# Low parts behind attention: from two engines to VectorE alone

## The chip, the cores and the metric

The kernel runs on one core of a Trainium2 chip. The metric is the device time of one execution in microseconds (us), as a median of several runs. A core has TensorE (PE, with its weight loads shown as PEld), VectorE (DVE), ScalarE (ACT), GpSimd (POOL) and SyncE (SP), which here only starts DMAs. Each engine takes its instructions in order.

## The reference, cut to what matters

One decoder block over 2048 positions of width 1024. The part that the change touches is the end: the output projection of the attention branch, the merge of the two branches, and the last projection.

```python
y_rnn = (hr * silu(z_rnn)) @ w_out_rnn
y_attn = (o * silu(z_attn)) @ w_out_attn
merged = sigmoid(g_r + bg_r) * y_rnn + sigmoid(g_a + bg_a) * y_attn
x = x + gate * (merged @ w_o)
return rms_norm(x, g_final)
```

## The kernel before, in words

**Split operands.** Every float32 operand of a matmul is held as a high part and a low part. ACT rounds the value to the high part (`hi_act`, L158). The low part is value minus high part, one elementwise subtraction on 128x512 elements, either on POOL (`lo_pool`, L164) or on DVE (`lo_dve`, L167). A product is then three matmuls (`mm3`, all on L150): high weight by high data, high weight by low data, low weight by high data, in that order.

**The jobs.** `steps` is a generator that runs eight jobs. Jobs 0 to 3 multiply `w_out_rnn` with the recurrent branch `yaT`, jobs 4 to 7 multiply `w_out_attn` with the attention branch `oT`; a job takes 512 positions. A job has 8 tiles of output rows (`t` counts them from 0 to 63, `m` within a job), a tile has 8 steps (`k`), and a step is one `mm3`, so a tile is 24 matmuls. The weights of a tile come in two halves, numbered `x = 2t` and `2t + 1`. Up to `t = 39` the steps are spread between the matmuls of attention. The last three jobs, `t = 40` (`TAIL0`) to `63`, come behind attention and are what this case is about: they take 192 steps (`LAST`).

**What a tile needs there.** The halves `x > 81` (`RAW`) are loaded unsplit from `wR` by SP (`load_w`, L1675) into one of six buffers, named S0 to S3, st3 and st4, five halves ahead; at the third step of half `x`, so six steps ahead of its use, `split_w(x + 2)` puts a `hi_act` on ACT and a low part on DVE (even `x`) or POOL (odd `x`). `split_y` does the same for the eight 128x512 blocks of `oT` of the next job; from job 6 on they are emitted around the steps given in `LATE_SPLIT_Y`, the last two of them in the first tile of the job that uses them. `evict` of tile `t - 1` comes in the second step of tile `t`: DVE multiplies the sum in PSUM with the gate block (L1716) and adds the recurrent branch's block (L1718); the two blocks are loaded by L1710 and the result is stored to `meT` by L1724, both on SP. The sums have two PSUM buffers, so tile `t + 1` can't start until tile `t - 1` is evicted.

**The output weights' rows.** The last projection is done afterwards by seven products for each pair of rows (`output_pair`), with operands B11, T2, T3, T1, B21, T4, B22 built from `w_o` while the last three jobs run. `build_rows(s, k)` is called for `s` = 14, 72, 100, 142 with `k` = 0 to 3 and hangs work on the steps `s` to `s + 21`: two products with the gate vector on POOL, four combinations on DVE, seven high parts on ACT and seven low parts. The rows come 512 KB at a time, two loads for each `k`, ten and seven steps before `s`; for `k` of 1 to 3 ACT's queue starts them, and each has to wait until the rows that lie in the same buffer (those of `k - 1`) have been read for the last time. The helpers:

```python
def load_rows(k, i):                                                      # L1852
    v[k, i] = t = stage(1 + i, [P, D])
    (nc.scalar if k else nc.sync).dma_start(t[:], w_o[...])               # L1854
def gate_rows(k, i):
    nc.gpsimd.tensor_tensor(v[k, i][:], v[k, i][:], v["gate"][:], ALU.mult)  # L1857
def combine(name, k, a, b, op):
    tt(part(name, k), part(a, k), part(b, k), op)                         # L1865, DVE
def low(name, k, lo):
    lo(B[name][1][:, k, :], part(name, k), B[name][0][:, k, :])           # L1871
```

T1, T2, T3 and T4 are made in place of B22, B11, B12 and B21 of the same rows, each from a difference or a sum of two parts. The whole stage is written out in emission order by hand (`manual_schedule`), so an engine's queue is the order of the code: within a step first the loads, the weight splits and the eviction, then the matmuls, then the splits of `oT`, and last what `build_rows` hung on the step.

Of the kernel before, what the change touches and what calls it, by code (L numbers as in the profile page):

```python
# [24 lines left out]
NB = 4  # L25
# [64 lines left out]
def decoder_block(ctx, tc, x, c, positions, g_norm, w_mod, b_mod, w_in, b_gate, conv_w, conv_b,  # L90
# [4 lines left out]
    def T(pool, shape, dt, tag, **kw):  # L95
        cnt[0] += 1
        return pool.tile(shape, dt, tag=tag, name=f"{tag}_{cnt[0]}", **kw)
# [59 lines left out]
    def hi_act(o, i):  # L157
        nc.scalar.activation(o, i, AF.Copy)  # L158
# [7 lines left out]
    def lo_dve(o, i, h):  # L166
        return nc.vector.tensor_tensor(o, i, h.bitcast(F32), ALU.subtract).ins  # L167
# [166 lines left out]
    n_w, n_y, W, Y0 = [0], [0], {}, {}  # L334
# [1323 lines left out]
    def steps(jobs):  # L1658
# [18 lines left out]
        def split_w(x):  # L1677
            if RAW < x < 2 * len(tiles):
                raw = W[x][:, 1].bitcast(F32)
                hi_act(W[x][:, 0], raw)  # L1680
                (lo_pool if x % 2 else lo_dve)(W[x][:, 1], raw, W[x][:, 0])

        def load_y(j, k, t):
            if j < len(jobs):
# [10 lines left out]
        def split_y(j, k):  # L1695
            if j < len(jobs):
                Y[j, k] = yh, yl = [T(fl, [P, CH], F32R, tag, bufs=NY) for tag in ("yh", "yl")]
                w, ys, n = jobs[j]
                t = Y0.pop((ys is yaT, n, k))
                hi_act(yh[:], t[:])  # L1700
                (lo_dve if k % 2 else lo_pool)(yl[:], t[:], yh[:])

        def load_g(t):
            j, m = tiles[t]
# [21 lines left out]
        for k in range(KT):  # L1726
            split_y(0, k)
        yield
        last = None
        for t, (j, m) in enumerate(tiles):  # L1730
            ps = T(pj, [P, CH], F32, "pj")
            for k in range(KT):
                x = 2 * t + k // KH
# [6 lines left out]
                if k % KH == 2 and x >= 2 * TAIL0:  # L1740
                    split_w(x + 2)
# [15 lines left out]
                yh, yl = Y[j, k]  # L1757
# [5 lines left out]
                x = m * KT + k - KT * (KT - 1)  # L1763
                j1 = j + 1
                if m == 0:
                    x, j1 = x + KT * KT, j
# [3 lines left out]
                for k1 in (LATE_SPLIT_Y if j1 > NB + 1 else SPLIT_Y).get(x, ()) if j1 else ():  # L1770
                    split_y(j1, k1)
# [70 lines left out]
    def on(n, fn, *args):  # L1842
        pend.setdefault(n, []).append((fn, args))
# [29 lines left out]
    def build_rows(s, k):  # L1873
        sub, add = ALU.subtract, ALU.add
        for d, fn, *args in (
            (0, gate_rows, k, 0), (6, gate_rows, k, 1), (6, high, "B11", k), (7, low, "B11", k, lo_dve),
            (12, combine, "T3", k, "B22", "B12", sub), (12, high, "B22", k), (13, combine, "T2", k, "B11", "T3", add),
            (14, high, "B21", k), (14, low, "B22", k, lo_pool), (15, low, "B21", k, lo_dve), (15, high, "T3", k),
            (16, high, "T2", k), (17, low, "T3", k, lo_pool), (17, combine, "T4", k, "B21", "T2", sub),
            (18, low, "T2", k, lo_dve), (18, combine, "T1", k, "B22", "T2", sub),  # L1880
            (19, high, "T4", k), (20, high, "T1", k), (21, low, "T4", k, lo_dve), (21, low, "T1", k, lo_pool)):
            on(s + d, fn, *args)

    A, ops = {}, {}
# [171 lines left out]
    with tc.manual_schedule():  # L2056
# [5 lines left out]
        for k, x in enumerate((14, 72, 100, 142)):  # L2062
            build_rows(x, k)
            for i in range(2):
                on(x - 10 + 3 * i, load_rows, k, i)
        on(LAST - 20, load_left, 0)
        for p in range(NP):
            for d, fn, args in left_events(p):
                x = 7 * p + d - 4
# [54 lines left out]
```

## Time and profile before

| | |
|---|---|
| time, median of 3 runs | 2229.85 us (2222.49 to 2233.4) |
| profiled execution, its own time | 2230.96 us |
| its span, first to last instruction | 2229.2 us |
| mean granted TensorE clock | 0.993 |
| busy over the span: PE, DVE, ACT, POOL | 97%, 65%, 58%, 49% |
| first matmul of tile 42, first matmul of the last projection | 1929.94, 2067.19 us |

The span is measured from the first to the last instruction, and the execution's own time has 1.76 us more around it. In a row of the timeline the first number is the start and the second the duration; a matmul's record is longer than its distance to the next one, because matmuls are pipelined. A group "x12 2.72" in the chain of waits is twelve matmuls that took 2.72 us from start to start of the next group, so 0.227 us each. A windows row gives the length of a stretch, then for each engine busy time and instructions, then clock, DMA share and rate.

### The profile page before, as it was taken

How to read it: one execution, taken by the hardware profiler on the slowest of the kernel's cores; microseconds unless marked ns; L12 is line 12 of the kernel's file. 1: busy time of each engine (PE TensorE's matmuls, PEld its weight loads, DVE VectorE, ACT ScalarE, POOL GpSimd, SP SyncE). 2: the span in 40 equal slices, each digit the busy share in tenths (PEclk: the TensorE clock that was granted, in tenths of full speed). 3: DMA queues.
4: the chain of work that ended last, by engine and by line, in shares of the span. 5: the costliest groups of instructions: out<-in, count | busy, mean ns of one | idle time of the engine just before them, and what ended most of it. 6: DMA issues, size and time to landing. Idle time of an engine off the chain costs nothing.

```text
span 2229.2 us, 34199 instructions
## 1 busy us (share of the span) xinstructions
PE 2170.3 (97%) x11326; PEld 1835.1 (82%) x11326; DVE 1454.1 (65%) x2475; ACT 1287.5 (58%) x2570; POOL 1095.9 (49%) x807
## 2 busy tenths in 40 slices
PE   8999999999999999999999999999999999998998
PEld 4998888888878998888788887888888988776886
DVE  5838888878556815545445342566777777788787
ACT  5637678668543627557546302777888887333333
POOL 2557677667557323222222102455665674566443
PEclk9999999999999999999999999999999999999999
DMA  8367887887999378888999988878887786997542
GB/s 278 115 214 257 286 288 268 297 285 266 323 286 306 111 224 271 284 291 276 303 300 302 358 302 272 255 235 261 267 265 234 236 261 208 299 309 237 185 164 110
DMA packets 412277, 573.41 MB, mean 257 GB/s; under 512 B 72422, under 2 KB 270274, under 8 KB 411076
## 3 DMA queue, kind: packets, MB, share of 16 engines
q1 hardware_dynamic: 369892, 442.82, 63.2%
q10 hardware_dynamic: 42016, 128.36, 15.0%
q8 instruction: 90, 1.47, 0.3%
q14 instruction: 87, 0.71, 0.1%
q0 software_dynamic: 192, 0.05, 0.0%
HBM read 352.99 MB, written 218.11 MB: 256 GB/s over the span
## 4 chain that ended last, share of the span: by engine, by line
PE 53%; DMA 5%; DVE 4%; issue 3%; ACT 2%; POOL 2%; SPq 1%; ACTq 0%; POOLq 0%; DVEq 0%
PE X L150 10%; PE V L150 10%; PE pj L150 9%; PE W L150 5%; PE Z L150 5%; PE Y L150 4%; PE sc L150 3%; PE o L150 3%; PE pg L150 1%; PE pT L1505 1%; PE pT L1518 1%; ACT pp L1421 1%; DMA R<-yaT 1%; POOL q L1382 1%; DMA S<-wD 1%
## 5 line engine op out<-in xcount | busy, mean ns | idle before, releaser
L164 POOL TENSOR_TENSOR S<-R,S 128x512 fp32r<-128x512 f32 x168 | 255.8, 1531 | 172.2 <-ACT S L158 66.7
L150 PE MATMUL pj<-yh,S 128*128 128x512 f32 x896 | 328.4, 407 | 10.1 <-POOL S L164 4.4
L150 PE MATMUL V<-T,S 128*128 128x512 f32 x1344 | 324.5, 390 | 4.0 <-DVE t L454 3.8
L150 PE MATMUL X<-T,S 128*128 128x512 f32 x1344 | 323.9, 390 | 1.4 <-POOL S L164 1.0
L150 PEld LDWEIGHTS V<-T,S 128*128 128x128 f32 x1344 | 251.8, 188 | 58.7 <-ACT S L158 2.6
L150 PEld LDWEIGHTS X<-T,S 128*128 128x128 f32 x1344 | 251.6, 188 | 55.2 <-POOL S L164 1.4
L150 PEld LDWEIGHTS pj<-yh,S 128*128 128x128 f32 x896 | 170.1, 190 | 43.9 <-POOL S L164 5.6
L164 POOL TENSOR_TENSOR S<-s,S 128x512 fp32r<-128x512 f32 x92 | 140.2, 1524 | 114.8 <-ACT S L158 74.3
L150 PE MATMUL pj<-yl,S 128*128 128x512 f32 x448 | 178.3, 398 | 3.0 <-DVE yl L167 2.5
L1421 ACT ACTIVATE pp<-pp,st 128x256 f32<-128x256 f32 (+3 forms) x256 | 133.5, 523 | 60.4 <-DVE st L1420 59.9
L150 PE MATMUL Z<-T,S 128*128 128x512 f32 x672 | 161.9, 390 | 0.0
L150 PE MATMUL Y<-T,S 128*128 128x512 f32 x672 | 161.8, 390 | 0.0
L150 PE MATMUL W<-T,S 128*128 128x512 f32 x672 | 161.7, 389 | 0.0
L150 PEld LDWEIGHTS W<-T,S 128*128 128x128 f32 x672 | 126.0, 188 | 27.0 <-issue 0.9
L167 DVE TENSOR_TENSOR ptl<-pT,pth 128x384 fp32r<-128x384 f32 (+1 forms) x160 | 97.9, 628 | 77.1 <-ACT pth L158 74.9
L150 PEld LDWEIGHTS Y<-T,S 128*128 128x128 f32 x672 | 125.9, 188 | 26.1
L150 PEld LDWEIGHTS Z<-T,S 128*128 128x128 f32 x672 | 125.8, 188 | 26.1
L164 POOL TENSOR_TENSOR s<-R,s 128x512 fp32r<-128x512 f32 x32 | 45.7, 1427 | 204.8 <-ACT s L158 169.8
L912 DVE SCALAR_TENSOR_TENSOR xc<-xr,par,xc 128x512 f32<-128x512 f32 x96 | 99.0, 1031 | 46.8 <-ACT xc L906 44.5
L158 ACT ACTIVATE S<-R 128x512 fp32r<-128x512 f32 x168 | 101.5, 622 | 45.5 <-DMA R<-in_w_in_dram 15.0
L1485 ACT ACTIVATE pp<-pp,M 128x256 f32<-128x256 f32 (+3 forms) x256 | 118.0, 523 | 9.6 <-DVE M L1608 9.6
L1420 DVE CUSTOM_DVE_ANT_0 pp<-sc,msk 128x256 f32<-128x256 f32 (+3 forms) x256 | 103.6, 447 | 29.1 <-PE sc L150 27.9
(418 smaller groups left out, 5005.5 us busy)
## 6 DMA issues: line engine op xcount, KB each, us to landing
sD<-S ACTq DMA_DIRECT2D x196, 512.0 KB, 4.4
S<-sD SPq DMA_DIRECT2D x196, 512.0 KB, 5.2
S<-wD SPq DMA_DIRECT2D x82, 512.0 KB, 5.3
R<-in_w_in_dram SPq DMA_DIRECT2D x136, 256.0 KB, 4.4
wD<-s ACTq DMA_DIRECT2D x64, 256.0 KB, 5.5
T<-in_w_mod_dram SPq DMA_DIRECT2D x8, 1024.0 KB, 11.7
vN<-ev SPq DMA_DIRECT2D x64, 128.0 KB, 2.7
zaT<-ev SPq DMA_DIRECT2D x32, 256.0 KB, 4.2
```

Of the source, the lines that this page charges most:

```text
L150: nc.tensor.matmul(o, lhsT=l, rhs=r, start=st, stop=sp, **kw)
L158: nc.scalar.activation(o, i, AF.Copy)
L164: nc.gpsimd.tensor_tensor(o, i, h.bitcast(F32), ALU.subtract)
L167: return nc.vector.tensor_tensor(o, i, h.bitcast(F32), ALU.subtract).ins
L912: nc.vector.scalar_tensor_tensor(xc, xr[:, i : i + CH], cw(i), xc, ALU.mult, ALU.add)
L1382: nc.gpsimd.tensor_copy(t[:, l], src.rearrange("p r (b a) -> p b r a", b=4))
L1420: nc.vector.tensor_tensor_reduce(pdst, s_ps, mask, 1.0, 3e38, ALU.add, ALU.min, m_)
L1421: nc.scalar.activation(pdst, pdst, AF.Exp, bias=m_, scale=-1.0, accum_out=l_)
L1485: nc.scalar.activation(pp, pp, AF.Copy, scale=w)
L1505: nc.tensor.transpose(pt[:, c0 + j * P : c0 + (j + 1) * P], pp[i][:, k * P : (k + 1) * P], ident)
L1518: nc.tensor.transpose(pt[:, c * P : (c + 1) * P], pp[:, half * P : (half + 1) * P], ident)
```

## The change

In the last three jobs and in the building of the output weights' rows, the low parts that POOL made are made by DVE. That covers the odd weight halves `x > 81`, the even blocks of `oT` of jobs 6 and 7 (job 5's stay where they were), and B22, T3 and T1 of each of the four `k`. POOL keeps the products of the rows with the gate vector. The place of each low part in the emission order stays the same, so it moves to the same point of another engine's queue. The splits of the left operands of the last projection (`left_split`) are not changed.

```diff
@@ split_w
-                (lo_pool if x % 2 else lo_dve)(W[x][:, 1], raw, W[x][:, 0])
+                lo_dve(W[x][:, 1], raw, W[x][:, 0])
@@ split_y
-                (lo_dve if k % 2 else lo_pool)(yl[:], t[:], yh[:])
+                (lo_dve if k % 2 or j > NB + 1 else lo_pool)(yl[:], t[:], yh[:])
@@ build_rows
-            (14, high, "B21", k), (14, low, "B22", k, lo_pool), (15, low, "B21", k, lo_dve), (15, high, "T3", k),
-            (16, high, "T2", k), (17, low, "T3", k, lo_pool), (17, combine, "T4", k, "B21", "T2", sub),
+            (14, high, "B21", k), (14, low, "B22", k, lo_dve), (15, low, "B21", k, lo_dve), (15, high, "T3", k),
+            (16, high, "T2", k), (17, low, "T3", k, lo_dve), (17, combine, "T4", k, "B21", "T2", sub),
             (18, low, "T2", k, lo_dve), (18, combine, "T1", k, "B22", "T2", sub),
-            (19, high, "T4", k), (20, high, "T1", k), (21, low, "T4", k, lo_dve), (21, low, "T1", k, lo_pool)):
+            (19, high, "T4", k), (20, high, "T1", k), (21, low, "T4", k, lo_dve), (21, low, "T1", k, lo_dve)):
```

## The prediction

> **What bounds the kernel now.** I read the page's engine line first, then the windows for the stage behind attention, then the timelines of PE, DVE, POOL and ACT in it.
>
> ```profile
> PE 2170.3 (97%) x11326; PEld 1835.1 (82%) x11326; DVE 1454.1 (65%) x2475; ACT 1287.5 (58%) x2570; POOL 1095.9 (49%) x807
> ```
>
> PE is at work 97% of the span, so only a place where PE stands still can give time back. The stage of the change has such a place.
>
> ```profile
> 1919.70:1929.94 10.24, 9.73 (x33) 7.40 (x34) 5.44 (x6) 3.42 (x6) 6.19 (x4) 0.83 1.04 385
> 1929.94:1985.85 55.91, 55.01 (x242) 44.90 (x241) 50.19 (x49) 21.71 (x38) 37.75 (x22) 1.00 0.91 305
> 1985.85:2034.43 48.58, 37.90 (x145) 28.39 (x144) 41.82 (x33) 18.51 (x33) 36.89 (x20) 0.93 0.78 248
> 2034.43:2067.35 32.92, 32.92 (x146) 27.11 (x145) 24.69 (x29) 8.60 (x15) 11.05 (x7) 1.00 0.78 237
> 2001.34:2025.15 23.81, 18.43 (x71) 13.68 (x70) 23.67 (x21) 12.75 (x23) 21.39 (x14) 0.93 0.83 277
> ```
>
> ```profile
> 1929.94 0.39 PE L150 MATMUL pj<-yh,st 128*128 128x512 f32 x1
> 1985.85 0.39 PE L150 MATMUL pj<-yh,S 128*128 128x512 f32 x1
> 2001.34 0.39 PE L150 MATMUL pj<-yh,st 128*128 128x512 f32 x1
> 2025.15 0.50 PE L150 MATMUL pj<-yl,S 128*128 128x512 f32 x1 [1.72 <-DVE yl L167]
> 2034.43 0.39 PE L150 MATMUL pj<-yh,S 128*128 128x512 f32 x1
> 2067.19 0.39 PE L150 MATMUL X<-B11h,st 128*128 128x512 f32 x1
> ...
> 2067.35 2.72 PE X L150 x12
> ```
>
> The windows are the first ten microseconds of job 5, then tiles 42 to 51, 52 to 57, and 58 to 63, and last a part of the third. Twelve matmuls take 2.72 us in the chain of waits, so a tile of 24 takes 5.44 us and a step 0.68. From the starts of tile 42 (1929.94), tile 52 (1985.85), tile 58 (2034.43) and the last projection (2067.19):
> tiles 42 to 51 took 55.91 us where ten tiles need 54.40: 1.5 lost.
> Tiles 52 to 57 took 48.58 where six need 32.64: 15.9 lost.
> Tiles 58 to 63 took 32.76 where 32.64 is needed: 0.1 lost.
> Together 17.5 us, nearly all in one stretch, and there POOL was busy for 36.89 of 48.58 us and DVE for 41.82. From 2001.34 to 2025.15 DVE was busy for 23.67 of 23.81 us.
>
> ```profile
> PE pj L150 <- POOL S L164: 4.4, 3, 2.6
> PE pj L150 <- DVE st L167: 2.2, 2, 1.6
> PE pj L150 <- ACT S L158: 2.0, 1, 2.0
> PE pj L150 <- DVE yl L167: 1.7, 1, 1.7
> PE pj L150 <- DVE S L167: 1.3, 2, 1.0
> ```
>
> PE's waits add up to 11.6 us. The rest of the 17.5 is slow clock after a wait (0.93 in the third window) and weight loads held up. Whom PE waits for is a low part in nearly every case, on either engine.
>
> ```profile
> 2006.17 0.68 DVE L167 TENSOR_TENSOR S<-S 128x512 fp32r<-128x512 f32 x1
> 2006.77 0.68 DVE L167 TENSOR_TENSOR B21l<-st,B21h 128x512 fp32r<-128x512 f32 x1
> 2011.48 0.68 DVE L1716 TENSOR_TENSOR R<-pj,fg 128x512 f32<-128x512 f32 x1
> 2012.19 1.04 DVE L1718 TENSOR_TENSOR R<-R,fg 128x512 f32<-128x512 f32 x1
> 2013.16 1.78 DVE L167 TENSOR_TENSOR yl<-T2l,yh 128x512 fp32r<-128x512 f32 x1
> 2014.86 1.77 DVE L167 TENSOR_TENSOR T4l<-st,T4h 128x512 fp32r<-128x512 f32 x1
> ...
> 2012.65 1.74 POOL L164 TENSOR_TENSOR T1l<-st,T1h 128x512 fp32r<-128x512 f32 x1
> 2014.35 1.74 POOL L164 TENSOR_TENSOR yl<-T3h,yh 128x512 fp32r<-128x512 f32 x1
> ```
>
> This is why. A 128x512 subtraction on DVE lasts 0.68 us with POOL idle and the next one starts 0.60 us later (2006.17, 2006.77). With POOL at work the same instruction lasts 1.77 us and they start 1.70 apart (2013.16, 2014.86), and so do POOL's (2012.65, 2014.35). The two engines finish a pair of low parts in 1.70 us; DVE alone would finish it in 1.20. The multiplication that reads PSUM (2011.48) keeps 0.68, and the addition behind it starts 0.71 later.
>
> **The change, part by part.**
>
> ```profile
> 1929.94:1985.85 55.91, 29.43 (x18) 1.00 0.91 305
> 1985.85:2034.43 48.58, 26.21 (x16) 0.93 0.78 248
> 2034.43:2067.35 32.92, 11.05 (x7) 1.00 0.78 237
> ```
>
> These are the low parts on POOL, 18 + 16 + 7 = 41 between tile 42 and the end of the stage, and all 41 go to DVE. The forty-second, half 83 in the first tile of job 5, comes before tile 42 and moves no term: DVE was busy there for 5.44 of 10.24 us. Each costs DVE 0.60 us, 25 us in all. DVE's whole list in the stage is then 24 evictions (0.71 + 0.60), 46 weight halves, 16 blocks of y, 28 low parts of rows and 16 combinations: 31 + 64 = 95 us at 0.60, against 131 us of PE for 24 tiles, to which the eight products left on POOL add at most 1.1 us for each DVE instruction that meets one. So DVE fits on the average, and what decides is its densest part.
>
> That part is tile 54 on, where the rows of k = 2 (steps 112 to 121) meet the blocks of y of job 7 (steps 117 to 129). In emission order DVE has from the start of tile 54 to the last block of y: two combinations, half, B22, B21, y0, T3, a combination, half, T2, a combination, y1, T4, T1, half, y2, y3, y4, half, y5, y6, y7, which is 22 instructions, and three evictions. That is 22 x 0.60 + 3 x 1.31 = 17.1 us. Before, 2001.34 to 2025.15 shows the same list done with POOL, and PE got its last block 23.8 us after the tile's start. Needed it is 15.9 us after it (step 23 and one matmul), and 7.9 of the 15.9 us lost are just that. Next on the list come the two halves of tile 57, needed 0.9 and 3.6 us after y7 and 0.6 us apart on DVE, so they follow in time once y7 does. If DVE starts its list with the tile, y7 comes 1.2 us late.
>
> ```profile
> 1985.83 0.68 DVE L1865 TENSOR_TENSOR st<-st,st 128x512 f32<-128x512 f32 x1
> 1987.71 0.69 DVE L167 TENSOR_TENSOR T4l<-st,T4h 128x512 fp32r<-128x512 f32 x1 [1.21 <-ACT T4h L158]
> ...
> 1986.67 0.34 ACTq L1854 DMA_DIRECT2D st<-in_w_o_dram  x1
> 1989.59 0.33 ACTq L1854 DMA_DIRECT2D st<-in_w_o_dram  x1
> 1990.02 1.67 ACT L158 ACTIVATE S<-S 128x512 fp32r<-128x512 f32 x3 [1.82 <-POOL T1l L164]
> ...
> 1988.28 1.27 POOL L164 TENSOR_TENSOR T1l<-st,T1h 128x512 fp32r<-128x512 f32 x1 [4.73 <-ACT T1h L158]
> 1994.81 2.40 POOL L1857 TENSOR_TENSOR st<-st,st 128x1024 f32<-128x1024 f32 x1 [2.80 <-DMA st<-in_w_o_dram]
> 1998.84 2.84 POOL L1857 TENSOR_TENSOR st<-st,st 128x1024 f32<-128x1024 f32 x1
> ```
>
> It may start later, because the first combination needs the second gate product of its rows. ACT's queue started the first load at 1986.67, when the last combination of the earlier rows had run (1985.83 + 0.68), and the second at 1989.59, when POOL's T1 low part ended; until then ACT made no weight halves, and PE stood for ACT's half made at 1990.02. From 1986.67 to the product at 1994.81 are 8.1 us of load. With DVE free of POOL I walk the end of its list for k = 1: tile 50 ends at 1985.85 - 5.44 = 1980.4, its eviction 1.3 later, then T3, a combination, a half, T2 and the last combination (5 x 0.60) end at 1984.7, T4 and T1 at 1985.9. Loads of 8.1 us, started then, land at 1992.8 and 1994.0; the products of 2.4 us, now without the half that POOL put between them (the gap from 1997.2 to 1998.84), end at 1995.2 and 1997.6. Tile 54 would start at 1985.85 + 10.88 = 1996.7, so the list starts 0.9 us late and y7 comes 2.1 us late in all. ACT, held by the second load until 1989.59, is free 3.6 us earlier, which covers PE's 2.0 us of waiting for the half of 1990.02 if that half's own load has landed; I leave 0.5 there. Clock: 0.93 over the third window is 3.4 us for some 11.6 us of waits, so 0.8 for these 2.6.
>
> Sum: tiles 52 to 57 lose 2.1 + 0.5 + 0.8 = 3.4 instead of 15.9. Tiles 42 to 51 lost 1.5 to waits for DVE's low parts; I take two thirds of it as won, 1.0. Tiles 58 to 63: nothing. The gain is 12.5 + 1.0 = 13.5 us. The profiled execution took 2230.96, 1.1 above the median of 2229.85; from it the change makes 2217.5, and for the median 2216.4. Since every short cut in this walk is in the change's favour, I give up half a microsecond of it and say 2217.
>
> Bounds: no more than the 17.5 us can go (2212.4), as the start of job 5 waits for ACT and for loads and stays. At the other end, if both gate products of k = 2 block DVE for their whole 2.4 us within the list, y7 comes 4.8 us later still, and the gain is 8.7 (2221).
>
> The Trainium skill has a rule against this change: its page "Perfetto Trace Analysis", section "Optimizing Scalar/DVE Operations", says that GpSimd and DVE share an SBUF port held as a lock, so that moving work between the two might not help. Taken so, the time would stay at 2230; the pairs above show the lock (1.77 against 0.68) and also that the pair costs more than two turns of DVE, so by the rows it does help.
>
> **Rivals.** *The loads become the bound.* The third window moved 248 GB/s x 48.58 us = 12.0 MB. In 32.64 us that is 369 GB/s. For: the second window ran at 305 with DMA at 0.91, and loads of 8 us occur. At 305 the 12.0 MB take 39.5 us, so 6.9 us stay lost instead of 3.4 and the gain is 10: 2220, from 2216 to 2224. Against: the first window carried 385 GB/s for ten microseconds, and loads are issued up to five halves ahead. The Trainium skill ("SBUF — State Buffer", section "A bandwidth-pool intuition that's wrong (but worth ruling out)") gives about 358 GB/s between HBM and a core; an estimate by that page would leave 12.0 / 0.358 = 33.5 us, 0.9 over PE's need, and the 385 of the first window goes past it.
>
> *The pair is one resource and nothing is won.* A low part on DVE would have to cost 0.85 us, half of a pair's 1.70, because it also waits for ACT's high part just before it. Then y7 comes as late as before, and only POOL's own waits (4.4 us on PE) shift: 2226 to 2230. This is the mechanism by which the Trainium skill's rule above, on "Perfetto Trace Analysis", would hold. Against: in the dense part ACT was busy for only 12.75 of 23.81 us, so highs come ahead of lows.
>
> *DVE stands behind a load: slower.* The low part of an odd half waits for ACT's high part, which waits for the half's load. On POOL that held up little; on DVE the next eviction stands behind it, and with two PSUM buffers PE behind that.
>
> ```profile
> L158 ACT ACTIVATE S<-S 128x512 fp32r<-128x512 f32 x27 | 16.4, 623 | 26.3 <-DMA S<-wR 14.6 <-PE pj L150 6.0 <-DVE T4l L167 3.6
> L158 ACT ACTIVATE st<-st 128x512 fp32r<-128x512 f32 x15 | 9.2, 619 | 14.2 <-DMA st<-wR 8.5 <-PE pj L150 5.8
> ```
>
> ACT waited 14.6 + 8.5 = 23.1 us for weight halves, so 11.6 for the odd ones. If DVE stands still for as long, and PE with it, and its freed time is eaten up by that, the time is 2229.85 + 11.6 = 2241. It decides once DVE's wait exceeds the six steps (4.1 us) between a split and its use. For: DMA at 0.91 to 1.04. Against: the even halves have stood on DVE all along and PE waited only 1.3 + 2.2 us for them.
>
> **How the numbers follow.** Forecast 0.64, loads 0.18, one resource 0.08, behind a load 0.10. Half a per cent is 11.1 us, about what a measurement of this kernel can tell from no change, since the three runs of before lie 10.9 us apart; so faster means below 2218.7. The forecast's own range is 2211 to 2222, of its chance 0.56 is below 2218.7; of the loads' 0.06; of the last rival 0.08 is 2241 or more and 0.02 short of it. Faster 0.62, same 0.30, slower 0.08. The range must leave out no more than 0.2: the last rival's 0.10 is left out above, and a little at each end; 2209 at the bottom takes in the bound of 2212.4 and a run-to-run spread of three, 2227 at the top takes in the loads and a part of the second rival.
>
> **What would show it.** Right: DVE's low parts at 0.68 us except beside the eight gate products, POOL with eight products of 2.4 to 2.8 us and nothing else between tiles 42 and 63, the first combination of k = 2 within 2 us of tile 54's start, tiles 52 to 57 in 36 to 38 us, PE's remaining waits on y lows of job 7 and on DVE alone. Wrong: tiles 52 to 57 over 42 us; DVE idle ahead of a weight half with "ACT S" as releaser and an eviction behind it; DMA at 1.0 through the stretch with ACT waiting for `wR` and PE for ACT; gate products that start later than 1995, relative to tile 53, than they do now.

## The result, and the profile after

| | before | after |
|---|---|---|
| time, median of 20 runs | 2229.61 us (2222.49 to 2237.95) | 2223.07 us (2217.67 to 2228.52) |
| ratio to before, with its 95% interval | | 0.9969 (0.9958 to 0.9979) |
| profiled execution and its span | 2230.96, 2229.2 us | 2226.09, 2224.3 us |
| tile 42 to the last projection | 137.25 us | 126.78 us |

The change makes the kernel faster by 6.5 us, 0.3%, with an interval from 4.7 to 9.4 us. That lies inside the range on record (2209 to 2227) and has the forecast sign, but it is half of the 13 us forecast, and it falls in the band of half a per cent around no change, which had been given 0.30; faster than that had been given 0.62.

The windows of the changed kernel, for tiles 42 to 51, 52 to 57 and 58 to 63, with busy time and instructions of PE, PEld, DVE, ACT and POOL, then clock, DMA share and rate; and the timeline rows of PE that bound them:

```profile
1935.53:1989.93 54.40, 54.40 (x242) 45.05 (x240) 46.01 (x67) 21.93 (x38) 8.30 (x4) 1.00 0.95 314
1989.93:2029.67 39.74, 35.73 (x146) 27.79 (x144) 35.12 (x46) 18.42 (x33) 10.31 (x4) 0.96 0.92 304
2029.67:2062.31 32.64, 32.64 (x146) 27.04 (x144) 23.40 (x37) 8.71 (x15) 0.00 (x0) 1.00 0.76 238
```

```profile
1935.53 0.39 PE L150 MATMUL pj<-yh,st 128*128 128x512 f32 x1
...
1989.93 0.39 PE L150 MATMUL pj<-yh,S 128*128 128x512 f32 x1
...
2001.81 0.39 PE L150 MATMUL pj<-yh,st 128*128 128x512 f32 x1
...
2029.67 0.39 PE L150 MATMUL pj<-yh,S 128*128 128x512 f32 x1
...
2062.31 0.39 PE L150 MATMUL X<-B11h,st 128*128 128x512 f32 x1
```

Tiles 42 to 51 now take 54.40 us and tiles 58 to 63 take 32.64, each exactly PE's need. Tiles 52 to 57 take 39.74 instead of 48.58 and still lose 7.1 us. POOL is busy for 8.30 us in the first stretch where it was 37.75. The groups of DVE show where its time came from (mean ns of one behind the busy time), first one row of the kernel before, then two of the changed one:

```profile
L167 DVE TENSOR_TENSOR S<-S 128x512 fp32r<-128x512 f32 x14 | 17.9, 1277 | 1.1 <-ACT S L158 1.1
```

```profile
L167 DVE TENSOR_TENSOR S<-S 128x512 fp32r<-128x512 f32 x28 | 20.3, 740 | 2.0 <-ACT S L158 2.0
L1718 DVE TENSOR_TENSOR R<-R,fg 128x512 f32<-128x512 f32 x22 | 19.9, 903 | 1.5 <-DMA fg<-mrT 0.7
```

A low part of a half in S0 to S3 takes 740 ns on average, where it was 1277; there are 28 instead of 14 and they take 20.3 us instead of 17.9. DVE does twice as many in nearly the same time.

### The profile page after: what moved, and what is told of

Its sections match the earlier page's. It is cut to its first block, busy times and chain, and to the rows that moved or that the text cites. A ratio compares the mean times of both kernels' runs of the same rounds, so it can differ in the third digit from the quotient of the medians.

```text
span 2224.3 us, 34201 instructions
## 1 busy us (share of the span) xinstructions
PE 2170.7 (98%) x11326; PEld 1836.2 (83%) x11326; DVE 1443.0 (65%) x2518; ACT 1287.1 (58%) x2570; POOL 1027.7 (46%) x764
## 4 chain that ended last, share of the span: by engine, by line
PE 53%; DMA 5%; issue 3%; DVE 3%; ACT 3%; POOL 2%; SPq 1%; ACTq 0%; POOLq 0%; DVEq 0%
PE pj L150 10%; PE X L150 10%; PE V L150 9%; PE W L150 5%; PE Z L150 5%; PE Y L150 4%; PE sc L150 3%; PE o L150 3%; PE pg L150 1%; PE pT L1505 1%; PE pT L1518 1%; ACT pp L1421 1%; DMA S<-wD 1%; POOL q L1382 1%; POOL kq L164 1%
## 5 line engine op out<-in xcount | busy, mean ns | idle before, releaser
L150 PE MATMUL Z<-T,S 128*128 128x512 f32 x672 | 161.9, 390 | 0.0
```

Of the source, the lines that this page charges most:

```text
L150: nc.tensor.matmul(o, lhsT=l, rhs=r, start=st, stop=sp, **kw)
```

## The experiments

The question was whether the gain comes from DVE running undisturbed by POOL (theory port, the prediction's own: an instruction of either engine takes longer beside one of the other) or from something else that the change did: low parts no longer queued behind others on POOL, or a shift of the whole stage (theory C). Later, where tiles 52 to 57 still lost time, it was DVE's dense list against the loads and against collisions with POOL's gate products.

The stage lengths below run from the first matmul of tile 42 to the first of the last projection, read from each profile's timeline. The three stretches in it are tiles 42 to 51 (PE needs 54.4 us), 52 to 57 (32.64) and 58 to 63 (32.64).

| kernel | stage, us | tiles 52 to 57, us | time, us | ratio to before |
|---|---|---|---|---|
| before (three profiles) | 137.25, 134.06, 137.26 | 48.58, 44.84, 48.70 | 2229.61 | 1 |
| after (two profiles) | 126.78, 126.77 | 39.74, 39.73 | 2223.07 | 0.9969 (0.9958 to 0.9979) |
| halves alone | 135.65 | 46.89 | 2228.90 | 0.9995 (0.9986 to 1.0004) |
| rows alone | 133.52 | 44.22 | 2229.98 | 1.0007 (0.9996 to 1.0018) |
| y blocks alone | 135.74 | 47.53 | 2232.02 | 0.9998 (0.9983 to 1.0013) |
| after, and POOL's work a second time | 150.44 | 52.49 | 2245.08 | 1.0070 (1.0052 to 1.0087) |
| after, k = 3 four steps later | 126.68 | 37.31 | 2220.26, one run | |
| after, rows from 14, 66, 94, 142 | 126.88 | 33.94 | 2221.46 | 0.9958 (0.9943 to 0.9973) |
| after, rows from 14, 56, 88, 142 | 124.07 | 32.70 | 2218.64 | 0.9949 (0.9935 to 0.9963) |
| the same, y blocks loaded earlier | 126.74 | 34.12 | 2219.98 | 0.9949 (0.9933 to 0.9966) |
| before, with both of these | 134.54 | 36.68 | 2225.07 | 0.9976 (0.9963 to 0.9988) |

The ratios are against the kernel before on the same chip, so times of different rows compare only roughly.

**Profiles again.** Both kernels unchanged, before twice and after once more.

> The kernel before, profiled a second time, to see how far its profile stands for its runs. In the first profiles the stage from tile 42 to the last projection took 137.3 us before and 126.8 us after, 10.5 us less, while the medians differ by 6.5 us and tile 42 started 5.6 us later in the profile of after. Theory A (the code ahead of the stage is the same, and its time varies from run to run): tile 42 starts anywhere from 1928 to 1938, and the stage again takes 135 to 139. Theory B (the first profile of before showed an unusually bad stage): the stage takes about 133, and the typical gain of the stage is the 6.5 us of the medians.

> The kernel before, profiled a third time, for the spread of its stage (137.3 and 134.1 us so far, while the changed kernel showed 126.8 twice). If its stage varies with the loads it takes 132 to 138; if the first profile was the exception it takes 133.5 to 134.5.

> The changed kernel, profiled a second time, for the same question. Theory A: the stage takes 126 to 128 again and tile 42 starts anywhere from 1928 to 1938, no later than in the kernel before. Theory B': the stage varies as well and takes about 130. Theory C (the change makes the part ahead of the stage slower by 4 us): tile 42 starts at 1934 to 1937 again, while the kernel before starts it near 1930.

Before, the stage took 134.06 and 137.26 us in these two profiles (runs of 2229.23 and 2228.52 us). The first lies between the ranges of theories A and B, the second where a stage that varies was expected; so the profile shown first was no exception, and why the stage varies is not shown. After, it took 126.77 (2218.91 us), the same as the first time to 0.01 us. Tile 42 started at 1931.41 and 1927.50 before and at 1928.39 after. Over the profiles of all kernels here, whose code ahead of the stage is the same but for the low part of half 83, it started from 1925.96 to 1936.95: at 1930.0 on the mean of the eight that make that low part on DVE, and at 1931.3 on the mean of the six others. The late start of the first profile of after (1935.53) is therefore no effect of the change, and theory C falls. The stage gained 9.4 us on the mean of three profiles, at the upper end of what the medians allow (4.7 to 9.4).

**POOL's work a second time.** Beside each low part that was moved, POOL subtracts the high part from itself into a tile of its own that nothing reads; the computed output does not depend on it.

```diff
                 lo_dve(W[x][:, 1], raw, W[x][:, 0])
+                if x % 2:
+                    again(W[x][:, 0].rearrange("p k m -> p (k m)"))    # lo_pool(dup, h, h)
...
+        if name in ("B22", "T3", "T1"):
+            again(B[name][0][:, k, :])
...
+                if k % 2 == 0 and j > NB + 1:
+                    again(yh[:])
```

> The changed kernel, and POOL makes in addition, at each of the 42 points where it made a low part before, a subtraction of the same size whose two inputs are the high part and whose result nobody reads. No engine waits for it, so POOL's queue can hold nobody up, but its accesses to SBUF are back. Theory port (POOL's subtractions slow DVE's while they run, 1.7 instead of 0.6 us): DVE's low parts show 1.7 us in the dense part again, each of POOL's 42 costs DVE some 1.07 us, 45 us over the stage, of which 15 to 25 us are not covered: 2235 to 2250, and tiles 52 to 57 over 50 us. Theory queue (the gain came from low parts no longer standing in POOL's queue behind the gate products and loads): the time stays at 2223 and tiles 52 to 57 at 40.

The time is 2245.08 us, 22 over the changed kernel's, and tiles 52 to 57 take 52.49 us. Windows of the three stretches, and the groups of DVE and POOL between 1930 and 2080:

```profile
1930.02:1994.16 64.14, 57.92 (x241) 45.49 (x240) 61.31 (x67) 21.36 (x38) 34.05 (x22) 0.97 0.83 268
1994.16:2046.65 52.49, 40.57 (x145) 30.00 (x144) 47.50 (x46) 17.89 (x33) 32.00 (x19) 0.87 0.70 229
2046.65:2080.46 33.81, 33.02 (x145) 26.95 (x144) 29.74 (x37) 9.11 (x16) 10.57 (x8) 1.00 0.76 232
```

```profile
L167 DVE TENSOR_TENSOR S<-S 128x512 fp32r<-128x512 f32 x28 | 33.4, 1208 | 1.8 <-ACT S L158 1.8
...
L164 POOL TENSOR_TENSOR dup<-S 128x512 bf16<-128x512 f32 x14 | 19.6, 1403 | 21.7 <-ACT S L158 21.3
```

No engine waits for these subtractions, and still DVE's low parts take 1208 ns on average instead of 740, PE's clock is 0.87 in the middle stretch, and PE loses 19.9 us there (52.49 against 32.64). The gate products do stand in POOL's queue behind these subtractions, but the profile shows no wait of DVE for POOL in the whole stage, and 18.0 of PE's 18.7 us of waits are for DVE's low parts. So what POOL costs is the time by which DVE's instructions get longer beside its own. The theory of POOL's queue is refuted as the main cause.

**The parts of the change, each alone.** Of the three changed places only one is kept in each kernel.

```diff
-                (lo_pool if x % 2 else lo_dve)(W[x][:, 1], raw, W[x][:, 0])
+                lo_dve(W[x][:, 1], raw, W[x][:, 0])           # halves alone
...
-            (14, high, "B21", k), (14, low, "B22", k, lo_pool), ...
+            (14, high, "B21", k), (14, low, "B22", k, lo_dve), ...    # rows alone; T3 and T1 likewise
...
-                (lo_dve if k % 2 else lo_pool)(yl[:], t[:], yh[:])
+                (lo_dve if k % 2 or j > NB + 1 else lo_pool)(yl[:], t[:], yh[:])   # y blocks alone
```

> The kernel before with only the odd weight halves moved to DVE (22 of the 42 low parts); POOL keeps the even y blocks and B22, T3 and T1 of the rows. The stage from tile 42 to the last projection took 137.3 and 134.1 us in two profiles of before, 126.8 and 126.8 after the whole change. Theory port (each low part on POOL costs DVE 1.07 us of standing still, each on DVE 0.60): a gain in proportion to the low parts moved in the dense part, 4 of the 11 that POOL had between 2001 and 2025, so the stage takes 130 to 133. Theory queue (the halves stood in POOL's queue behind the gate products, PE waited 4.4 us for them and that was it): nearly the whole gain is here, 127 to 128.5.

> The kernel before with only B22, T3 and T1 of the rows moved to DVE (12 of the 42 low parts). Theory port: 3 of the 11 low parts between 2001 and 2025, the stage takes 131 to 134. Theory list (DVE is the engine that ends last in tiles 54 to 56, so three more low parts there make it worse if POOL keeps the rest): 136 to 139.

> The kernel before with only the even y blocks of jobs 6 and 7 moved to DVE (8 of the 42 low parts). The halves alone gave 0.9995 of the time, the rows alone 1.0007, the whole change 0.9969. Theory port with a list (every part shortens DVE's list in tiles 54 to 56 by 0.47 us for each low part moved, four in each case or three for the rows, so the parts give some 2 us each and add up to the whole): ratio 0.998 to 1.000, tiles 52 to 57 take 43 to 46 us. Theory y (the blocks of job 7 are what PE waits for last, so they carry nearly the whole): ratio 0.9965 to 0.998, tiles 52 to 57 at 40 to 42.

None of them made a difference beyond its interval, and the sum of three is far from the whole, 0.9969. The expectation of shares by number of low parts was wrong, for the halves (135.65 us against 130 to 133) and the y blocks (tiles 52 to 57 at 47.53 against 43 to 46); the rows came to 133.52, in their range, with no gain in time. The ratio of the y blocks alone (0.9998) lay in the range of that theory (0.998 to 1.000). Only in part is it seen why the single parts gave so little. Timelines of POOL and DVE with the halves alone:

```profile
2016.82 1.72 POOL L164 TENSOR_TENSOR yl<-T4h,yh 128x512 fp32r<-128x512 f32 x1
2018.50 5.60 POOL L1857 TENSOR_TENSOR st<-st,st 128x1024 f32<-128x1024 f32 x2
...
2019.01 2.86 DVE L167 TENSOR_TENSOR S<-S 128x512 fp32r<-128x512 f32 x1
2021.79 2.85 DVE L167 TENSOR_TENSOR yl<-T1l,yh 128x512 fp32r<-128x512 f32 x1
2025.89 0.68 DVE L167 TENSOR_TENSOR yl<-T4l,yh 128x512 fp32r<-128x512 f32 x1
```

With fewer low parts in its queue POOL came to the two gate products of k = 3 earlier, at 2018.5, in the middle of DVE's dense list, and DVE's half and y block there took 2.86 and 2.85 us instead of 0.68. In the kernel before, POOL started them at 2024.51, only as the list's last block of y was being made (tile 54 at 2001.34, the block's end at 2025.1, so 23.8 us after the tile's start). With the halves alone that block ended 25.5 us after the start of tile 54 (2026.57, 2001.04): what the low parts saved was spent there. With the y blocks alone it ended after 23.1 us (2029.37, 2006.27): DVE had four blocks more in its list, and seven of its instructions there still took 1.76 to 1.80 us beside POOL's, where it had been nine.

**The gate products of k = 3.** The same happens after the whole change, less severely. Timelines of POOL and DVE of the changed kernel:

```profile
2018.10 2.74 POOL L1857 TENSOR_TENSOR st<-st,st 128x1024 f32<-128x1024 f32 x1 [15.94 <-DVE yl L167]
...
2018.52 0.68 DVE L1716 TENSOR_TENSOR R<-pj,fg 128x512 f32<-128x512 f32 x1
2019.23 2.15 DVE L1718 TENSOR_TENSOR R<-R,fg 128x512 f32<-128x512 f32 x1
2021.31 0.68 DVE L167 TENSOR_TENSOR yl<-T4l,yh 128x512 fp32r<-128x512 f32 x1
```

An addition of an eviction took 2.15 us instead of 0.69, ahead of the last block of y. So the rows of k = 3 were built four steps later.

```diff
-        for k, x in enumerate((14, 72, 100, 142)):
+        for k, x in enumerate((14, 72, 100, 146)):
```

> The changed kernel with the rows of k = 3 built four steps later, from 146, their loads from 136 and 139. In the profile of the changed kernel POOL, which has nothing else to do, made the first gate product of k = 3 at 2018.1, in the middle of DVE's dense list, and the addition of an eviction at 2019.2 took 2.15 us instead of 0.69. Theory collision: the product comes after the list, the last block of y of job 7 is ready 1.5 us earlier, tiles 52 to 57 take 37.5 to 38.5 us instead of 39.7. Theory list alone (the list is late by its own length and its late start): they stay within 0.5 us of 39.7.

POOL made the products at 2018.37 in this profile, but 20.7 us after the start of tile 54 instead of 16.3, and tiles 52 to 57 took 37.31 us, 2.4 less, a little more than the theory of the collision had said. The stage as a whole was 126.68 us, no shorter, since 1.3 us were lost in tiles 49 and 50 and 1.0 in 58 and 59, where the changed kernel had lost nothing; why is not shown.

**The peak of DVE's list parted.** The two middle numbers of the same line were changed, first to 66 and 94.

```diff
-        for k, x in enumerate((14, 72, 100, 142)):
+        for k, x in enumerate((14, 66, 94, 142)):
```

> The changed kernel with the rows of k = 1 built from step 66 instead of 72 and those of k = 2 from 94 instead of 100, so that the dense ends of the two (steps 78 to 87 and 106 to 115) lie between the y blocks of job 6 (until step 65) and of job 7 (from step 117). DVE's work is the same, only its peak is lower. Theory list (what is left of the loss, 7.1 us in tiles 52 to 57, is DVE's list of tile 54 on, 22 subtractions and combinations and three evictions that end 4.3 us after PE needs the last block): most of it goes, tiles 52 to 57 take 34 to 36 us, the time is 4 to 6 us under the changed kernel, about 2218. Theory loads (the stretch moves 12 MB and is bound by them): tiles 52 to 57 stay at 38 to 40 us and the time at 2222 to 2224.

Tiles 52 to 57 went to 33.94 us, as the list's theory had it, but the stage stayed at 126.88 and the time at 2221.46, above the 2218 expected: tile 48 and the two behind it lost 5.9 us. That was not foreseen. So the rows were moved to 56 and 88.

```diff
+        for k, x in enumerate((14, 56, 88, 142)):
```

> The changed kernel with the rows built from 14, 56, 88 and 142. Moving k = 1 to 66 and k = 2 to 94 took tiles 52 to 57 from 39.7 to 33.9 us, but tiles 48 to 50 lost 5.9 us instead of none, for the low parts of job 6's blocks (steps 53 to 65) then met the gate products and loads of k = 1. Here the dense ends (68 to 77 and 100 to 109) are clear of both sets of blocks, but the loads of k = 1 (steps 46 and 49) come while the blocks of job 6 are loaded. Theory list: both losses go, the stage takes 120.5 to 123 instead of 126.8, the time is 4 to 6 us under the changed kernel, 2217 to 2219. Theory loads: the loads of k = 1 delay the blocks of job 6 and tiles 44 to 50 lose 3 to 6 us, the stage stays at 124 to 127.

The same stretches in windows:

```profile
1931.09:1989.82 58.73, 56.12 (x242) 44.51 (x241) 46.22 (x70) 23.73 (x42) 12.67 (x6) 1.00 0.92 312
1989.82:2022.52 32.70, 32.70 (x146) 26.95 (x145) 29.32 (x43) 16.07 (x29) 5.88 (x3) 1.00 1.01 340
2022.52:2055.16 32.64, 32.64 (x146) 27.03 (x144) 24.16 (x37) 9.34 (x16) 1.83 (x1) 1.00 0.77 244
```

Tiles 52 to 57 took 32.70 us, PE's need to 0.06 us, at a DMA share of 1.01 and 340 GB/s. That speaks for DVE's list as the bound of this stretch and against the loads, with one reserve: the loads of k = 2 now go out ahead of tile 52, and the stretch moves 11.1 MB (340 GB/s x 32.70 us) where it moved 12.1 in the changed kernel (304 x 39.74). The changed kernel's own profile settles it: from 1999.22 to 2022.00 DVE was busy for 22.68 of 22.78 us, so its list waited for no load. The stage took 124.07 us, which is in the range of theory loads (124 to 127) and not in that of theory list (120.5 to 123). In tiles 48 to 50 4.3 us were still lost, and the loads of k = 1 looked like the cause. In the next kernel the y blocks are loaded 16 steps earlier as well.

```diff
-    LATE_LOAD_Y = {2 * k - 20: [k] for k in range(KT)}
+    LATE_LOAD_Y = {2 * k - 36: [k] for k in range(KT)}
```

> The changed kernel with the rows built from 14, 56, 88 and 142, and the y blocks of jobs 6 and 7 loaded 16 steps earlier (from step 20 and step 84). With the rows at these steps alone, tiles 52 to 57 took 32.70 us, no loss, and the 4.3 us left were in tiles 48 to 50, where DVE had stood for 2.8 and 1.7 us for gate and branch blocks and ACT 8.1 us for a half, at a DMA share of 0.96. Theory loads in tiles 44 to 47 (the loads of k = 1 and of job 6's blocks fall together): parted, the loss there goes, the stage takes 120 to 122 us and the time is 2213 to 2217. Theory list (DVE's y blocks and the halves are too many for tile 48 in any case): the stage stays at 123 to 125.

Timelines of POOL and DVE ahead of tile 48:

```profile
1954.73 5.21 POOL L1857 TENSOR_TENSOR st<-st,st 128x1024 f32<-128x1024 f32 x2 [24.29 <-ACT yh L158]
...
1955.15 2.53 DVE L1718 TENSOR_TENSOR R<-R,fg 128x512 f32<-128x512 f32 x1 [0.21 <-DMA fg<-mrT]
1957.61 2.88 DVE L167 TENSOR_TENSOR yl<-T2l,yh 128x512 fp32r<-128x512 f32 x1
```

Neither range for the stage was met: it took 126.74 us. The loss in tiles 48 to 50 stayed (4.8 us), and 1.5 us were lost in tile 54 and 0.7 in tiles 58 and 59. DVE no longer stood for loads as it had, but the gate products of k = 1 now ran together for 5.21 us, and the two DVE instructions beside them took 2.53 and 2.88 us just ahead of job 6's blocks. That the loads were the cause was therefore not shown; moving the loads moved the products. A version with the products elsewhere was not tried. Last, the kernel before with the lines of both of these diffs, and its low parts on two engines as they were:

> The same steps of the rows and of the y loads, but the low parts shared between DVE and POOL as in the kernel before. Theory port (a pair of low parts costs 1.70 us on two engines and 1.20 on one, wherever it stands): the pairs still hold PE up, less than before since the peaks are parted, the stage takes 125 to 131 us and the time is 4 to 9 us over the same steps with all low parts on DVE. Theory peak (only the peak in tiles 54 to 56 counted, and any engine serves once it is spread): the stage takes 120 to 123 us in both.

With the same steps and loads but the low parts on two engines the stage took 134.54 us, 7.8 more than with all on DVE, and the ratio was 0.9976 against 0.9949. The stage is longer than either theory had said (125 to 131, 120 to 123), but the time is 5.1 us over the other, within the 4 to 9 of theory port, and the peak alone would have made both alike. So theory port holds. The steps alone are worth 0.24%, the change of engines about as much on top.

Rows from 14, 56, 88 and 142 with all low parts on DVE had the shortest stage and the lowest time: 0.9949 of before, 2218.64 us, a ratio that the version with the earlier loads shares. Its interval (0.9935 to 0.9963) overlaps the changed kernel's, so that it beats before is shown, and that it beats the change is likely.

## Why the prediction was right, and half too large

**Port.** Right. The pair of low parts on two engines at 1.70 us against 1.20 on DVE was the working core, and the kernel with POOL's subtractions doubled shows it alone. PE no longer waits for POOL. These are the waits of PE in the changed kernel between tile 42 and the last projection (in all, how often, the longest, us):

```profile
PE pj L150 <- DVE yl L167: 2.2, 1, 2.2
PE pj L150 <- DVE S L167: 1.3, 1, 1.3
PE pj L150 <- ACT S L158: 0.6, 2, 0.4
```

The waits for low parts on DVE are those of job 7's blocks and a half, as forecast.

**Tiles 42 to 51 and 58 to 63.** The first were forecast to keep 0.5 of 1.5 us lost and kept none; the last had nothing to give.

**Tiles 52 to 57.** Here a step failed: 3.4 us left were forecast and 7.1 are left. The 39.74 us that they took lie between the 36 to 38 that were to show the prediction right and the 42 that were to show it wrong. Term by term, with the timelines of ACT, DVE and POOL around the rows of k = 2 and the list of tile 54, the waits of PE there, and a window from tile 55 to tile 58:

```profile
1989.71 0.33 ACTq L1854 DMA_DIRECT2D st<-in_w_o_dram  x1
1990.10 0.63 ACT L158 ACTIVATE T4h<-st 128x512 fp32r<-128x512 f32 x1 [5.42 <-DVE st L1865]
1992.09 0.33 ACTq L1854 DMA_DIRECT2D st<-in_w_o_dram  x1
1992.52 1.67 ACT L158 ACTIVATE S<-S 128x512 fp32r<-128x512 f32 x3 [1.27 <-DMA fg<-gaT]
...
1988.95 0.69 DVE L1865 TENSOR_TENSOR st<-st,st 128x512 f32<-128x512 f32 x1
1990.76 0.69 DVE L167 TENSOR_TENSOR T4l<-st,T4h 128x512 fp32r<-128x512 f32 x1 [1.12 <-ACT T4h L158]
1991.37 0.68 DVE L167 TENSOR_TENSOR T1l<-st,T1h 128x512 fp32r<-128x512 f32 x1
...
1999.82 2.88 DVE L167 TENSOR_TENSOR B11l<-st,B11h 128x512 fp32r<-128x512 f32 x1
...
2003.23 0.68 DVE L1865 TENSOR_TENSOR st<-st,st 128x512 f32<-128x512 f32 x1
...
1996.35 2.39 POOL L1857 TENSOR_TENSOR st<-st,st 128x1024 f32<-128x1024 f32 x1 [17.27 <-DMA st<-in_w_o_dram]
1999.36 2.80 POOL L1857 TENSOR_TENSOR st<-st,st 128x1024 f32<-128x1024 f32 x1 [0.61 <-DVE R L1718]
...
1993.21 0.50 PE L150 MATMUL pj<-yh,S 128*128 128x512 f32 x1 [0.40 <-ACT S L158]
...
2015.04 0.74 PE L150 MATMUL pj<-yh,S 128*128 128x512 f32 x2 [1.30 <-DVE S L167]
...
2022.04 0.59 PE L150 MATMUL pj<-yl,S 128*128 128x512 f32 x1 [2.16 <-DVE yl L167]
...
2007.25:2029.67 22.42, 18.81 (x74) 14.42 (x72) 20.03 (x28) 10.23 (x19) 5.12 (x2) 0.92 0.87 283
```

y7's lateness was forecast at 2.1 us and measured at 4.3: its low part ended at 2021.99, and PE, with tile 54 begun at 2001.81, needed it at 2017.68. Three parts make it up. The list's own excess was nearly right: leaving out the collision named next, it took 17.3 us from 2003.23 on, against 17.1, which is 1.4 us too long instead of 1.2. The collision with k = 3's gate product (the addition at 2019.23, shown above) cost 1.5 us. And the list started 1.4 us after the tile instead of 0.9.

That late start is a collision as well. The second gate product of k = 2 ended at 2002.16, only 0.35 us after the tile's start. But DVE, which worked without a gap, made B11's low part beside this product, and it took 2.88 us (1999.82) instead of 0.68. Without that the list could have started with the product's end, some 1.0 us earlier; this is an estimate from these rows. The collisions with gate products are thus about 2.5 of the 4.3 us.

This is the step that failed. The sum put these collisions at nothing, and the text put them at no more than 1.1 us for each DVE instruction; the rows show 1.5 and 2.2. The bound of 2221 held only those with k = 2's products, and the prediction did not ask what an idle POOL would do next with k = 3's. The size could have been read from the kernel before, where the same low part beside the same product had taken as long:

```profile
1999.35 2.88 DVE L167 TENSOR_TENSOR B11l<-st,B11h 128x512 fp32r<-128x512 f32 x1
```

The walk to the loads had a mistake in it too, which shorter loads made up for. T1's low part was put at the start of tile 52, and it ended 2.1 us after it (1992.05 against 1989.93). On ACT the high part of T4 is queued behind the load that waits for the last combination (1989.71, 1990.10), so DVE's T4 waited 1.12 us for it, and the second load went out at 1992.09. The loads themselves were shorter than the 8.1 us assumed, 6.6 from 1989.71 to the product at 1996.35. PE's wait for ACT's half shrank from 2.0 to 0.4 us, but tiles 52 and 53 lost 1.0 us where 0.5 was left.

The clock term was 0.8 and is 1.8: 0.92 over the 22.42 us from 2007.25 to 2029.67. Together 4.3 + 1.0 + 1.8 = 7.1.

**From stage to time.** The stage won 10.5 us in the first pair of profiles, where the walk said 13.5, and 9.4 against three profiles of before: the first profile, on which the sum was made, was 1.1 us worse than their mean. The medians moved by 6.5. What comes behind the stage took 161.9 to 162.0 us in all five profiles of the two kernels, so the 3 us between would have to lie ahead of the stage or in executions that were not profiled. They can't be told from the spread ahead of the stage; they stay open.

**The range.** The forecast's own part of it ended at 2222. The measured 2223 lies in the part that was taken in for the loads and the one resource, and it was neither of these that put it there; that the range held is in part luck.

**Rivals.** Loads as the bound: not in this stretch, where DVE worked without a gap for 22.68 of 22.78 us. One resource: refuted, since low parts on DVE start 0.61 us apart (1990.76, 1991.37) and not 0.85, though it describes the time of the single parts well. The Trainium skill's "Perfetto Trace Analysis", section "Optimizing Scalar/DVE Operations", says that shifting work between GpSimd and DVE might not help; each part alone agrees with that (0.9995, 1.0007, 0.9998), and the whole does not (0.9969). Behind a load: DVE waited for ACT's halves for 4.7 us in the stage, no longer than 2.0 at once, under the 4.1 from which it would have decided. DVE's waits in the changed kernel, same columns as PE's above:

```profile
DVE st L167 <- ACT st L158: 2.7, 2, 2.0
DVE S L167 <- ACT S L158: 2.0, 3, 1.1
```

## What to carry to other kernels

Two elementwise engines can slow each other by more than sharing the work between them saves: measure a pair side by side and two turns on one engine first (1.70 and 1.20 us here). When work is taken off an engine, look at what then moves ahead in its queue and what that meets; here an early gate product cost DVE 1.5 to 2.2 us at the worst place. Where an engine's average load is fine, walk its densest stretch instruction by instruction, with the queues of the other engines in it, and part the peak: this brought nearly as much as the change of engines (0.24% with both engines kept, against 0.31%).

## What was not expected of the hardware

An instruction on DVE that meets one of POOL's lost up to 1.1 us (1.77 against 0.68) when POOL's was 512 elements wide and up to 2.2 us (2.88 against 0.68) when it was 1024 wide, so in these rows the loss grew with the length of POOL's instruction. And PE's clock fell around short waits: windows of the changed kernel around the waits of 1.30 us (2015.04) and 2.16 us (2022.04).

```profile
2015.00:2018.00 3.00, 2.96 (x13) 2.46 (x14) 3.00 (x6) 3.00 (x7) 0.00 (x0) 1.00 0.98 323
2018.00:2021.00 3.00, 1.88 (x9) 1.23 (x7) 2.97 (x3) 0.17 (x1) 2.74 (x1) 1.00 0.97 335
2021.00:2024.00 3.00, 1.96 (x5) 1.58 (x6) 2.96 (x6) 0.79 (x2) 0.75 (x1) 0.72 0.68 219
2024.00:2027.00 3.00, 3.00 (x11) 2.35 (x11) 3.00 (x3) 1.00 (x2) 1.63 (x1) 0.71 0.72 203
2027.00:2029.67 2.67, 2.67 (x14) 2.20 (x12) 0.38 (x1) 0.63 (x1) 0.00 (x0) 1.00 0.55 150
```

The clock was 1.00 behind the first wait and 0.72 and 0.71 for the six microseconds from 2021 on, during and behind the second. Whether the second alone would have done it is not shown.
